# Layer 1's queries: one transposed operand with the high part above the low, and a second one copied from it by DMA

## The chip, the cores and the metric

The kernel runs on one core of one Trainium2 chip. The metric is the device time of one execution in microseconds (us). The engines are TensorE (PE, with its weight loads PEld apart), VectorE (DVE), ScalarE (ACT), GpSimd (POOL) and SyncE (SP), which issues the DMA transfers.

## The reference

A block of two layers works on 512 latent tokens and 256 context tokens of width 1024. Layer 0 is a windowed and a dense grouped-query attention side by side, layer 1 a differential attention; each is followed by a SwiGLU network. The part in question is layer 1's attention, with 8 heads of two halves (`a` = 0, 1) of 64 dimensions:

```python
def heads(p, use_rope):
    q, k, v = jnp.split(p, [qs, 2 * qs], axis=-1)
    q = _rms(q.reshape(b, n, HEADS_C, 2, d), qn)
    k = _rms(k.reshape(b, n, HEADS_C, 2, d), kn)
    if use_rope:
        q, k = _rope(q, cos, sin), _rope(k, cos, sin)
    return q, k, v.reshape(b, n, HEADS_C, 2 * d)
...
s = jnp.einsum('bqhad,bkhad->bhaqk', qb, k).astype(jnp.float32) * scale
p = jax.nn.softmax(s, axis=-1)
a = (p[:, :, 0] - lam * p[:, :, 1]).astype(v.dtype)
return jnp.einsum('bhqk,bkhe->bqhe', a, v)
```

Queries come from the 512 latent tokens, keys and values from all 768.

## The kernel before, in words

All numbers are float32. Where a product must be exact enough, an operand is split into a high part of the faster type `F32R`, which ACT's copy makes, and a low part, the difference; the product is then taken in several terms.

Layer 1's attention works in tiles of 128 tokens (4 latent query tiles, 6 key tiles) and in heads. A head is projected (`Proj1.sums`, with the products at L465) in two half-sums per tile, with weights of 4 units of 256 rows each. `weight1` loads a unit by three transfers (L365, `wir`) into one of two buffers with the tag `raw`, ACT casts its high part (L370, `wih`) and POOL makes its low part (L371, `wil`); five units have room at a time, so a unit's cast waits until PE has used an older one, and a load waits until POOL has finished the unit before the last. All `wir` loads go through SP's queue, which issues in order.

`Proj1.finish` copies a tile's projection out of its accumulator (ACT, L677), normalizes and rotates it, and splits queries (`qd`, L685 on ACT and L686 on DVE) and keys (`kd`, L688 on ACT and L689 on POOL). It returns `transposes`, which is called some steps later: PE turns the queries (L696) and the keys (L702), and ACT copies them out of PSUM (L698, L703). The split key operand `kT` holds the high part in partitions 0 to 63 and the low part in 64 to 127. The query operand `qt` exists twice: once with the high part in both halves of the partitions, once with the low part in both. So the two products L715 and L716 of `attend1` give high x high + high x low and low x high + low x low: all four terms. For this `qd` holds each part twice, and four transposes are made per tile.

`attend1` is a generator with three parts: the scores with the row maximum (L718, `mx`), the exponential (L720, `e`) and the combination of both halves (L727); the transposes of the weights (L734, `ppt`) with copies (L737, L739, `PT`); and the products with the values (L744, `av`) with the normalized output (L746 to L751).

The loop at L1673 goes through 32 pairs of head and query tile. In each pass come the scores of pair i, a half-sum of a later head, the transposes of pair i - 1, another half-sum, the values of pair i - 1, and, as they come due, the transposes of projected tiles (`turned`; a tile comes due five half-sums after its projection, so the queries of a head are turned two to four passes before their use). A tile `qt` has one of five buffers. PE keeps the order in which this is written (`manual_schedule` for PE alone); the instructions of the other engines and of SP's queue are ordered by the framework's planner, from its own estimates.

Of the kernel before, what the change touches and what calls it, by code (L numbers as in the profile page):

```python
# [12 lines left out]
F32R = mybir.dt.float32r  # L13
# [6 lines left out]
P = 128  # L20
# [7 lines left out]
HD = 64  # L28
# [23 lines left out]
def bc(ap, pos, n):  # L52

    dims = [list(d) for d in ap.ap]
    return AP(ap.tensor, ap.offset, dims[:pos] + [[0, n]] + dims[pos:])
# [8 lines left out]
def backbone(es: ExitStack, tc: tile.TileContext, x, c, ctx, c_ctx, mod_w, mod_b, norm_mix_w, norm_ffn_w,  # L64
# [3 lines left out]
    nc = tc.nc  # L68
# [24 lines left out]
    def acc_tile(name, n=512, one=None):  # L93

        if one is None:
            one = turn["acc"] = 1 - turn["acc"]
        return p_1.tile([P, 512], F32, name=name, tag=f"acc{one}")[:, :n]
# [4 lines left out]
    def tr_tile(name, shape, dt=F32, one=None):  # L102
        if one is None:
            one = turn["tr"] = 1 - turn["tr"]
        return p_1.tile(shape, dt, name=name, tag=f"tr{one}")
# [10 lines left out]
    def f32(ap):  # L116
        return ap.bitcast(F32)
# [13 lines left out]
    identr = cp.tile([P, P], F32R, name="identr")  # L131
# [24 lines left out]
    def rsqrt(ss, n, inv, tag):  # L156

        r = small.tile([P, n], F32, name="rs_" + tag, tag="rs_" + tag)
        nc.gpsimd.tensor_scalar(r, ss, inv, EPS, ALU.mult, ALU.add)
        nc.gpsimd.tensor_tensor(r, r, neghalf[:, :n], ALU.pow)  # L160
        return r
# [319 lines left out]
    def weights0(b, wp, subs, new_tile=raw_tile, loads=((0, 1), (), (2,), (3,))):  # L481
# [3 lines left out]
        for u in range(4):  # L485
# [13 lines left out]
            subs[u % len(subs)].tensor_sub(lo, raw, f32(hi))  # L499
            yield hi, lo  # L500

    def tables0(j, tabs, wp):
        tabs[j] = rope_tables(wp, *((ev_qn_a[0], ev_kn_a[0]) if j == 0 else (ev_qn_b[0], ev_kn_b[0])))

# [152 lines left out]
    class Proj1:  # L657
# [14 lines left out]
        def finish(self, t, ps):  # L672

            n, wp, kT, qs = self.width(t), self.wp.pool, self.kT, self.qs
            m, h0 = (n - P) // HD, 0 if t < NTX else 2
            raw = wp.tile([P, 384], F32, name="qkv", tag="qkv", bufs=4)
            nc.scalar.copy(raw[:, :n], ps[:, :n])  # L677
            nc.gpsimd.tensor_copy(self.vv[:, t, :], raw[:, n - P:n])
            y, r = rotate_all(raw[:, :n - P], h0, m, t, self.wc, self.tb, wp)
            nc.gpsimd.tensor_tensor(y, y, bc(r, 2, HD), ALU.mult)  # L680
            nq = m - 2
            if nq:
                qd = wp.tile([P, 2, 2, 2, HD], F32R, name="qd", tag="qd", bufs=3)
                yb = bc(y[:, 0:2], 2, 2)
                nc.scalar.copy(qd[:, 0], yb)  # L685
                nc.vector.tensor_sub(qd[:, 1], yb, f32(qd[:, 0]))  # L686
            kd = wp.tile([P, 2, 2, HD], F32R, name="kd", tag="kd", bufs=3)
            nc.scalar.copy(kd[:, :, 0, :], y[:, nq:nq + 2])  # L688
            nc.gpsimd.tensor_sub(kd[:, :, 1, :], y[:, nq:nq + 2], f32(kd[:, :, 0, :]))  # L689

            def transposes():
                if nq:
                    pt = tr_tile("qpt", [P, 2, 2, P], F32R)
                    for j in range(2):
                        for a in range(2):
                            nc.tensor.transpose(pt[:, j, a, :], qd[:, j, a].rearrange("p a d -> p (a d)"), identr)  # L696
                    qt = self.qp.tile([P, 2, 2, P], F32R, name="qt", tag="qt", bufs=5)
                    nc.scalar.copy(qt, f32(pt))  # L698
                    qs[t] = qt
                pk = tr_tile("kpt", [P, 2, P], F32R)  # L700
                for a in range(2):
                    nc.tensor.transpose(pk[:, a, :], kd[:, a].rearrange("p a d -> p (a d)"), identr)  # L702
                nc.scalar.copy(kT[:, :, t * P:(t + 1) * P], f32(pk))  # L703
            return transposes

    def attend1(h, t, state, o_t, nlam, subln, mp):
        qs, kT, vv = state.qs, state.kT, state.vv
        mx = small.tile([P, 2], F32, name="mx", tag="mx")
        sm = small.tile([P, 2], F32, name="sm", tag="sm")
        E = []  # L710
        for a in range(2):
            sc = p_sc.pool.tile([P, 1024], F32, name="sc", tag="sc", bufs=2)
            for s0, k0, k1 in ((256, SEQ, TOK), (512, 0, SEQ)):
                so = sc[:, s0:s0 + k1 - k0]
                nc.tensor.matmul(so, qs[t][:, 0, a, :], kT[:, a, k0:k1], start=True, stop=False)  # L715
                nc.tensor.matmul(so, qs[t][:, 1, a, :], kT[:, a, k0:k1], start=False, stop=True)  # L716
            s = sc[:, 256:256 + TOK]
            nc.vector.tensor_reduce(mx[:, a:a + 1], s, AX.X, ALU.max, negate=True)  # L718
            e = mp.tile([P, TOK], F32, name="e", tag="e", bufs=PBUF)
            turn["exp"] = nc.scalar.activation(e, s, AF.Exp, bias=mx[:, a:a + 1], accum_out=sm[:, a:a + 1])  # L720
            E.append(e)
        rc = small.tile([P, 2], F32, name="rc", tag="rc")
        nc.vector.reciprocal(rc, sm)

        rt = small.tile([P, 1], F32, name="rt", tag="rt")
        nc.vector.scalar_tensor_tensor(rt, sm[:, 0:1], nlam, rc[:, 1:2], ALU.mult, ALU.mult)
        nc.vector.scalar_tensor_tensor(E[0], E[1], rt, E[0], ALU.mult, ALU.add)  # L727
        yield
        vt = [4, 5, 0, 1, 2, 3]
        pts = []  # L730
        for g0, m in ((0, 4), (4, 2)):
            pt = tr_tile("ppt", [P, 4, P])
            for a in range(m):
                nc.tensor.transpose(pt[:, a, :], E[0][:, (g0 + a) * P:(g0 + a + 1) * P], ident)  # L734
            PT = mp.tile([P, 4, P], F32, name="PT", tag="PT", bufs=3)
            if g0:
                nc.vector.tensor_copy(PT[:, :m], pt[:, :m])  # L737
            else:
                nc.scalar.copy(PT, pt)  # L739
            pts += [PT[:, a, :] for a in range(m)]  # L740
        yield
        av = acc_tile("av", P, one=1)
        for kc, PT in enumerate(pts):
            nc.tensor.matmul(av, PT, vv[:, vt[kc], :], start=kc == 0, stop=kc == NT - 1)  # L744
        oc = o_t[t][:, h * P:(h + 1) * P]
        nc.scalar.activation(oc, av, AF.Copy, scale=rc[:, 0:1])  # L746
        ss = small.tile([P, 1], F32, name="oss", tag="oss")
        o1 = mp.tile([P, P], F32, name="o1", tag="o1", bufs=2)
        nc.scalar.activation(o1, oc, AF.Square, accum_out=ss)
        r = rsqrt(ss, 1, 1.0 / P, "o")  # L750
        nc.vector.scalar_tensor_tensor(oc, oc, r, subln, ALU.mult, ALU.mult)  # L751
# [405 lines left out]
    wp = Pool("mw0", "right")  # L1157
# [5 lines left out]
    for t in CTX_FIRST:  # L1163
# [4 lines left out]
        for g in range(2):  # L1168
            pt = tr_tile("npt", [P, 4, P])
# [120 lines left out]
    if True:  # L1290
        for i, (b, t) in enumerate(steps):
            j = i % NT
# [37 lines left out]
            if t == 0:  # L1330
# [13 lines left out]
                wp = Pool("w0", "right")  # L1344
# [219 lines left out]
    wp = Pool("mw1", "right")  # L1564
# [44 lines left out]
    if True:  # L1609
# [117 lines left out]
        wp = Pool("w1", "right")  # L1727
# [203 lines left out]
```

## Time and profile before

| | before |
|---|---|
| median of 3 runs (lowest to highest) | 1695.23 us (1695.23 to 1698.65) |
| the profiled execution: its span (no other time of it is given) | 1695.6 us |
| mean granted clock of TensorE | 0.992 |
| TensorE busy | 1631.5 us, 96% |
| layer 1's attention, from its first scores to the last | 1002.2 to 1293.5 us |
| SP's loads inside 1010 to 1250 us | 63 of 128 KB |

Busy time of the engines is the time in which they execute; matmuls overlap one another, so the distance of their starts, not the length of one, says what one costs. In a group's row stand its line, engine, operation, output and inputs, the shape, the count, the busy time, the mean length in ns, and the idle time before it with what ended it. In a row of the timeline stand the start, the length, the engine and the line; "x4" merges four neighbours, and brackets hold idle time before it. A row of the waits gives total, number and longest.

### The profile page before, as it was taken

The page shows a single profiled execution, that of the slowest core. Times are in us where ns is not written, and L with a number is a line of the kernel's source. Part 1 is how long each engine was busy: PE and PEld are TensorE (multiplying, and loading weights), DVE is VectorE, ACT ScalarE, POOL GpSimd, SP SyncE. Part 2 cuts the span into 40 slices and gives each one's busy share as a digit, 9 for nine tenths or more (in the row PEclk, how much of TensorE's full clock was granted, in tenths as well). Part 3 has the DMA queues.
Part 4 walks back from the last instruction along what each step waited for, and adds up shares of the span by engine and source line. Part 5 has one row for each costly group of instructions (what it writes and reads, how often), then busy time and mean ns, then how long its engine had stood idle before and what let it go on. Part 6 is the DMA issues. An engine that isn't in the chain of part 4 may idle for free. (4 is left out here: it accounts for less than half of the span.)

```text
span 1695.6 us, 28585 instructions
## 1 busy us (share of the span) xinstructions
PE 1631.5 (96%) x10390; PEld 1468.6 (87%) x10390; DVE 1146.7 (68%) x2014; ACT 937.0 (55%) x2011; POOL 696.4 (41%) x867
## 2 busy tenths in 40 slices
PE   6999999899999999999999989999999999999998
PEld 3977787677999999998777889999988899999887
DVE  3765656754799887767767656666666598887434
ACT  5565555745456665545554456666666555555320
POOL 2665554321346554412413366666664242221000
PEclk8999999999999999999999999999999999999999
DMA  9222221411455555439966311111112433331431
GB/s 319 69 71 74 70 70 50 164 60 38 129 167 172 164 159 162 134 108 347 296 184 189 99 43 38 48 42 44 50 45 97 125 93 102 111 101 57 137 99 62
DMA packets 218108, 194.64 MB, mean 115 GB/s; under 512 B 20016, under 2 KB 202864, under 8 KB 217968
## 3 DMA queue, kind: packets, MB, share of 16 engines
q1 hardware_dynamic: 217616, 192.62, 36.8%
q8 instruction: 81, 1.33, 0.3%
q14 instruction: 59, 0.48, 0.1%
q10 hardware_dynamic: 352, 0.21, 0.0%
HBM read 179.92 MB, written 12.87 MB: 114 GB/s over the span
## 5 line engine op out<-in xcount | busy, mean ns | idle before, releaser
L901 ACT CAST wbh<-wr 128x512 fp32r<-128x512 f32 x170 | 104.9, 621 | 130.2 <-PE p L933 73.4
L933 PE MATMUL p<-hT,wbh 128*128 128x256 f32 (+1 forms) x752 | 154.5, 299 | 0.0
L465 PE MATMUL inps<-wih,hT 128*128 128x384 f32 x512 | 144.2, 344 | 7.3 <-ACT qkv L677 7.3
L911 POOL TENSOR_TENSOR wbl<-wr,wbh 128x512 fp32r<-128x512 f32 x43 | 60.0, 1396 | 173.6 <-ACT wbh L901 173.6
L933 PEld LDWEIGHTS p<-hT,wbh 128*128 128x128 f32 x752 | 121.9, 191 | 0.2
L911 DVE TENSOR_TENSOR wbl<-wr,wbh 128x512 fp32r<-128x512 f32 x127 | 107.7, 858 | 21.0 <-ACT wbh L901 16.8
L933 PE MATMUL p<-hT,wbl 128*128 128x256 f32 (+1 forms) x376 | 111.9, 298 | 0.0
L933 PE MATMUL p<-t,wbh 128*128 128x384 f32 (+1 forms) x480 | 111.3, 318 | 0.0
L604 POOL TENSOR_SCALAR Pt<-Pt,rc 128x256 f32<-128x256 f32 (+3 forms) x96 | 74.6, 788 | 89.3 <-DVE rc L601 83.1
L231 POOL TENSOR_TENSOR modp<-modp 128x512 f32<-128x512 f32 x40 | 57.4, 1436 | 114.3 <-ACT modp L230 114.3
L465 PEld LDWEIGHTS inps<-wih,hT 128*128 128x128 f32 x512 | 93.3, 188 | 10.6 <-ACT qkv L677 9.7
L933 PE MATMUL p<-hTt,wbh 128*128 128x256 f32 (+1 forms) x480 | 101.0, 302 | 0.0
L887 POOL TENSOR_TENSOR wr<-wr 128x512 f32<-128x512 f32 x40 | 61.6, 1540 | 89.8 <-DVE ws L892 85.8
L933 PE MATMUL p<-b,wbh 128*128 128x384 f32 x368 | 93.8, 336 | 0.2 <-DVE c L961 0.2
L901 ACT CAST wbh<-ws 128x512 fp32r<-128x512 f32 x120 | 69.4, 579 | 43.1 <-PE p L933 29.0
L224 DVE SCALAR_TENSOR_TENSOR ma<-modw,cols,ma 128x256 f32<-128x256 f32 x140 | 89.2, 637 | 2.3
L592 ACT ACTIVATE Pt<-sc,nm 128x256 f32<-128x256 f32 (+3 forms) x96 | 67.6, 707 | 35.3 <-DVE nm L588 16.9
L465 PE MATMUL inps<-wil,hT 128*128 128x384 f32 x256 | 86.0, 336 | 0.0
L933 PEld LDWEIGHTS p<-t,wbh 128*128 128x128 f32 x480 | 82.9, 189 | 0.0
L911 DVE TENSOR_TENSOR wbl<-ws,wbh 128x512 fp32r<-128x512 f32 x120 | 81.7, 681 | 1.7 <-ACT wbh L901 1.6
L933 PEld LDWEIGHTS p<-hTt,wbh 128*128 128x128 f32 x480 | 78.3, 191 | 3.1 <-ACT modp L230 1.6
L230 ACT ACTIVATE modp<-modw,cols 128x256 f32<-128x256 f32 x160 | 68.4, 500 | 18.0 <-POOL ma L236 10.1
(355 smaller groups left out, 5217.9 us busy)
## 6 DMA issues: line engine op xcount, KB each, us to landing
modw<-in_mod_w_dram SPq DMA_DIRECT2D x96, 512.0 KB, 5.2
wr<-in_ffn_w_in_dram SPq DMA_DIRECT2D x176, 256.0 KB, 2.9
wdr<-in_ffn_w_out_dram SPq DMA_DIRECT2D x66, 512.0 KB, 3.7
wir<-in_od_w_in_dram SPq DMA_DIRECT2D x96, 128.0 KB, 2.3
hidm<-hid SPq DMA_DIRECT2D x44, 192.0 KB, 1.9
hr<-hidm SPq DMA_DIRECT2D x22, 192.0 KB, 3.5
x<-in_x_dram SPq DMA_DIRECT2D x8, 512.0 KB, 3.5
wir<-in_ev_w_in_dram SPq DMA_DIRECT2D x16, 256.0 KB, 3.5
```

The costliest lines, as they stand in the source:

```text
L224: nc.vector.scalar_tensor_tensor(acc, w[:, k], scale[k], acc, ALU.mult, ALU.add)
L230: nc.scalar.activation(pr[:, k], w[:, k], AF.Copy, scale=scale[k])
L231: nc.gpsimd.tensor_add(pr[:, 0:2], pr[:, 0:2], pr[:, 2:4])
L465: nc.tensor.matmul(ps, hs[j][:, k, :], ws[k // 2][z][:, k % 2, c0:c1], start=(k, j, z) == (0, 0, 0), stop=(k, j, z) == (KT - 1, 1, 0))
L592: turn["exp"] = nc.scalar.activation(p[:, :n], s, AF.Exp, bias=nm[:, c1], accum_out=sm[:, c1])
L604: nc.gpsimd.tensor_scalar(p[:, :n], p[:, :n], rc[:, hh:hh + 1], 1.0, ALU.mult, ALU.mult)
L887: nc.gpsimd.tensor_sub(w, raw[f, "G1"], w)
L901: nc.scalar.copy(hi, w)
L911: (nc.gpsimd if name == "G2" else nc.vector).tensor_sub(lo, raw[need[n]], f32(hi))
L933: nc.tensor.matmul(ps, w[:, k, :], H[b][h][:, k, :], start=first and k == 0 and q == 0, stop=final and k == 3 and q == 2, skip_group_check ...
```

## The change

`qd` now holds each query once, its high part in the first 64 and its low part in the last 64 columns, as `kd` always did. Two transposes per tile, one for each half-head, give the first operand, `qt[:, 0]`, with high above low. The second operand, `qt[:, 1]`, has low above high; two DMA transfers on SP's queue copy it from the first inside SBUF, each moving 64 partitions of 1 KB (64 KB). The products stay the same two: high x high + low x low, and low x high + high x low.

A swap isn't issued where the tile is turned but one tile later: `halves_swapped` keeps the newest one back, and `swapped()` at the start of each pair's scores issues what is left.

```diff
+    swaps = []
+
+    def swapped(left=0):
+        while len(swaps) > left:
+            to, src = swaps.pop(0)
+            for j in range(2):
+                nc.sync.dma_start(f32(to[HD * (1 - j):HD * (2 - j)]), f32(src[HD * j:HD * (j + 1)]))
+
+    def halves_swapped(to, src):
+        swaps.append((to, src))
+        swapped(1)
...
-                qd = wp.tile([P, 2, 2, 2, HD], F32R, name="qd", tag="qd", bufs=3)
-                yb = bc(y[:, 0:2], 2, 2)
-                nc.scalar.copy(qd[:, 0], yb)
-                nc.vector.tensor_sub(qd[:, 1], yb, f32(qd[:, 0]))
+                qd = wp.tile([P, 2, 2, HD], F32R, name="qd", tag="qd", bufs=3)
+                nc.scalar.copy(qd[:, :, 0, :], y[:, 0:2])
+                nc.vector.tensor_sub(qd[:, :, 1, :], y[:, 0:2], f32(qd[:, :, 0, :]))
...
-                    pt = tr_tile("qpt", [P, 2, 2, P], F32R)
-                    for j in range(2):
-                        for a in range(2):
-                            nc.tensor.transpose(pt[:, j, a, :], qd[:, j, a].rearrange("p a d -> p (a d)"), identr)
+                    pt = tr_tile("qpt", [P, 2, P], F32R)
+                    for a in range(2):
+                        nc.tensor.transpose(pt[:, a, :], qd[:, a].rearrange("p a d -> p (a d)"), identr)
                     qt = self.qp.tile([P, 2, 2, P], F32R, name="qt", tag="qt", bufs=5)
-                    nc.scalar.copy(qt, f32(pt))
+                    nc.scalar.copy(qt[:, 0], f32(pt))
+                    halves_swapped(qt[:, 1], qt[:, 0])
                     qs[t] = qt
...
         E = []
+        swapped()
         for a in range(2):
```

On PE nothing moves: two query transposes stand wherever four stood. The planner orders the other engines anew. On SP's queue, in the passes of the middle heads, the loads of the weight units stood in a row before (the number behind `wir` is one unit's buffer: 12389 is unit 3 of one head, 12921 to 12945 are units 0 to 3 of the next):

```order
L365 DMA wir_12381<-in_od_w_in_dram 128x2x128 x3
L365 DMA wir_12389<-in_od_w_in_dram 128x2x128 x3
L365 DMA wir_12921<-in_od_w_in_dram 128x2x128 x3
L365 DMA wir_12929<-in_od_w_in_dram 128x2x128 x3
L365 DMA wir_12937<-in_od_w_in_dram 128x2x128 x3
```

Now the swaps of the query tiles (L508, a pair for each tile) stand between them:

```order
L365 DMA wir_12381<-in_od_w_in_dram 128x2x128 x3
L508 DMA qt_12029<-qt_12029 64x256 x2
L365 DMA wir_12389<-in_od_w_in_dram 128x2x128
L508 DMA qt_12289<-qt_12289 64x256 x2
L365 DMA wir_12389<-in_od_w_in_dram 128x2x128 x2
L508 DMA qt_12332<-qt_12332 64x256 x2
L365 DMA wir_12921<-in_od_w_in_dram 128x2x128 x3
L365 DMA wir_12929<-in_od_w_in_dram 128x2x128 x3
L508 DMA qt_12470<-qt_12470 64x256 x2
L365 DMA wir_12937<-in_od_w_in_dram 128x2x128 x3
L508 DMA qt_12585<-qt_12585 64x256 x2
```

Unit 3's load is split by the swap of the next head's query tile 0, and unit 0 follows behind that of tile 1. On ACT, at the same place of a middle head, stood before (the first `wih` here is unit 3's cast, the second that of unit 0 of the head after):

```order
L420 ACTIVATE sq<-qkv 128x256
L370 CAST wih<-wir 128x768
L720 ACTIVATE e,sm<-sc,mx 128x768
L685 CAST qd<-qy 128x256
L688 CAST kd<-qy 128x2x64
L370 CAST wih<-wir 128x768
L739 COPY PT<-ppt 128x512
L720 ACTIVATE e,sm<-sc,mx 128x768
L677 COPY qkv<-inps 128x256
```

and now stands, with the lines of the changed file (11 to 12 higher):

```order
L420 ACTIVATE sq<-qkv 128x256
L370 CAST wih<-wir 128x768
L732 ACTIVATE e,sm<-sc,mx 128x768
L696 CAST qd<-qy 128x2x64
L699 CAST kd<-qy 128x2x64
L751 COPY PT<-ppt 128x512
L732 ACTIVATE e,sm<-sc,mx 128x768
L370 CAST wih<-wir 128x768
L689 COPY qkv<-inps 128x256
```

The copy of PT and the second exponential moved ahead of the second cast.

## The prediction

> **What bounds the kernel now.** I read the page's first block first, then the busy time by stretch around the changed place.
>
> ```profile
> span 1695.6 us, 28585 instructions
> PE 1631.5 (96%) x10390; PEld 1468.6 (87%) x10390; DVE 1146.7 (68%) x2014; ACT 937.0 (55%) x2011; POOL 696.4 (41%) x867
> ```
>
> TensorE (PE) is busy in 96% of the span. The change touches only layer 1's attention; its three stretches (start, six even heads, end) are, with the columns PE, PEld, DVE, ACT and POOL busy, granted clock, DMA share and GB/s:
>
> ```profile
> 975.00:1010.00 35.00, 29.80 (x194) 27.91 (x193) 17.85 (x35) 19.19 (x48) 24.66 (x39) 1.00 0.19 52
> 1010.00:1250.00 240.00, 234.42 (x1657) 225.68 (x1656) 151.80 (x312) 157.47 (x409) 159.79 (x254) 1.00 0.15 42
> 1250.00:1300.00 50.00, 44.50 (x286) 39.13 (x285) 37.81 (x68) 35.43 (x82) 30.48 (x48) 0.97 0.31 95
> ```
>
> In the middle 240 us PE idles only 5.6 us, at full clock; every other engine is at two thirds, and the DMA engines at 15%. So time goes where PE instructions go, except where PE already waits. The waits of that middle stretch (total, times, longest):
>
> ```profile
> PEld inps L465 <- ACT qkv L677: 4.8, 6, 0.9
> PE inps L465 <- ACT qkv L677: 3.4, 6, 0.6
> PEld inps L465 <- POOL wil L371: 2.6, 6, 1.2
> ACT wih L370 <- PE inps L465: 4.8, 12, 0.6
> ACT wih L370 <- DMA wir<-in_od_w_in_dram: 2.6, 2, 1.4
> PE av L744 <- ACT PT L739: 0.7, 2, 0.6
> ```
>
> Both of PE's recurring waits come six times, once per head: one for the copy of the projection out of its accumulator, one for the low part of a weight unit. The second decides what a saved PE instruction is worth.
>
> **The PE term.** The timeline of PE in one head:
>
> ```profile
> 1098.51 0.54 PE L696 MATMUL qpt<-identr,qd 128*128 128x128 f32 x4
> 1098.88 0.33 PE L702 MATMUL kpt<-identr,kd 128*128 128x128 f32 x2
> 1099.05 0.41 PE L465 MATMUL inps<-wih,hT 128*128 128x384 f32 x1
> ...
> 1101.20 0.47 PE L696 MATMUL qpt<-identr,qd 128*128 128x128 f32 x4
> 1101.50 0.34 PE L702 MATMUL kpt<-identr,kd 128*128 128x128 f32 x2
> 1101.67 0.35 PE L715 MATMUL sc<-kT,qt 128*128 128x256 f32 x1
> ```
>
> Matmuls overlap, so the cost is start to start: four query transposes take 0.37 and 0.30 us, two key transposes behind them 0.17. Dropping two of four saves 0.15 (half of 0.30) to 0.185 (half of 0.37); I take 0.165. With 8 heads of 4 query tiles that is 32 x 0.165 = 5.3 us (4.8 to 5.9) if every group lay on the path. The Trainium skill ("TensorE: Matmul & The Clock Gate", section "Wait — 56ns, not 53.3ns?") has back-to-back matmuls of 128 columns 56 ns apart at full clock; by it, an estimate, the 64 would be 3.6 us. The trace does not agree here: 0.17 for two is 85 ns each, and the row decides.
>
> **Half of it is already owed to a wait.** Each head's four groups come at about 1098.5, 1101.2, 1109.1 and 1118. Behind the first two, PE meets this:
>
> ```profile
> 1105.45 0.40 PE L465 MATMUL inps<-wih,hTc 128*128 128x256 f32 x2
> 1105.69 0.28 PE L465 MATMUL inps<-wil,hTc 128*128 128x256 f32 x1
> 1105.81 0.39 PE L465 MATMUL inps<-wih,hTc 128*128 128x256 f32 x2
> 1106.29 0.39 PE L465 MATMUL inps<-wil,hTc 128*128 128x256 f32 x1
> ...
> 1107.73 1.60 PE L744 MATMUL av<-vv,PT 128*128 128x128 f32 x12 [0.58 <-ACT PT L739]
> ```
>
> Two products take 0.24 us (1105.45 to 1105.69); the next two take 0.48, so 0.24 is idle, since the low part of weight unit 3 ends at 1104.39 + 1.85 = 1106.24. POOL, busy with six short operations and unit 2 between them, runs without a pause from unit 1 to unit 3:
>
> ```profile
> 1097.32 1.98 POOL L371 TENSOR_TENSOR wil<-wir,wih 128x768 fp32r<-128x768 f32 x1 [1.92 <-ACT wih L370]
> ...
> 1104.39 1.85 POOL L371 TENSOR_TENSOR wil<-wir,wih 128x768 fp32r<-128x768 f32 x1
> ```
>
> Its start waits for ACT's cast, and that cast for PE to give back a weight buffer (the 12 waits in the list above), before the two groups; the order of POOL between these two rows is unchanged. So 2 x 0.165 saved in front of that wait only lengthens it. What counts is the other two groups: 6 heads x 0.33 = **2.0 us**.
>
> **What ACT and DVE give.** Groups of the attention stretch (busy, mean ns):
>
> ```profile
> L698 ACT CAST qt<-qpt 128x512 fp32r<-128x512 f32 x32 | 18.7, 586 | 2.7 <-PE qpt L696 2.6
> L703 ACT CAST kT<-kpt 128x256 fp32r<-128x256 f32 x48 | 18.2, 378 | 1.2 <-PE kpt L702 1.2
> L685 ACT CAST qd<-qy 128x256 fp32r<-128x256 f32 x32 | 13.0, 406 | 23.4 <-POOL qy L680 23.4
> L688 ACT CAST kd<-qy 128x128 fp32r<-128x128 f32 x46 | 13.7, 298 | 14.4 <-POOL qy L680 14.2
> L427 DVE TENSOR_TENSOR qy<-qkv,rc 128x128 f32<-128x128 f32 x14 | 4.7, 339 | 3.0 <-POOL kd L689 1.5 <-issue 0.6 <-POOL vv L678 0.5
> ```
>
> The copy of qt goes from 586 to 378 ns, the cast of qd from 406 to 298: 0.316 x 32 = 10 us of ACT, nearly all in idle time. On a path to PE lies the DVE subtraction between a tile's two row maxima, which sets the second exponential and then the accumulator copy that PE awaits:
>
> ```profile
> 1092.34 0.41 DVE L686 TENSOR_TENSOR qd<-qy,qd 128x256 fp32r<-128x256 f32 x1
> ```
>
> At half the elements it is like the 339 ns row or a little under: 0.1 less, once per head, 6 x 0.1 = **0.6 us**. The new order also puts ACT's copy of PT ahead of the cast of the next head's first unit, which waits for its DMA; that was the 0.58 us in the row at 1107.73 and the whole entry of 0.7: **0.7 us**.
>
> **The two ends.** Three waits there:
>
> ```profile
> 992.39 0.37 PE L702 MATMUL kpt<-identr,kd 128*128 128x128 f32 x2 [0.86 <-POOL kd L689]
> 1002.13 0.28 PE L288 MATMUL gps<-cst,modc 128*8 128x128 f32 x1 [0.41 <-ACT kT L703]
> 1269.79 0.75 PE L696 MATMUL qpt<-identr,qd 128*128 128x128 f32 x4 [0.76 <-ACT qt L698]
> ```
>
> Head 0's groups mostly precede waits on POOL (0.86), and their saving is lost as above; ACT's shorter copy in front of the wait at 1002.13 (0.21) and its group (0.17) count, with the shorter cast of qd (0.11) twice: 0.6. Head 7's four groups give 0.66, and 0.21 at 1269.79, where PE waits for the copy of qt itself; some goes into the latencies of the last tiles: 0.7. Together **1.3 us**. Gains: 2.0 + 0.6 + 0.7 + 1.3 = 4.6.
>
> **What is added.** Each tile issues two transfers of 64 KB on SP's queue: 64 in all. Latency first:
>
> ```profile
> L715 PE MATMUL sc<-kT,qt x128: 274/378/400, 1002.2 to 1293.5; 128*128 128x256 f32 x64, 128*128 128x512 f32 x64
> L698 ACT CAST qt<-qpt x32: 573/587/594, 989.4 to 1270.6; 128x512 fp32r<-128x512 f32 x32
> L365 SPq DMA_DIRECT2D wir<-in_od_w_in_dram x63: 367/469/1345, 1020.0 to 1220.9; - x63
> DMA to landing us min/median/max: 2.1/2.3/4.0
> ```
>
> The first copy ends near 990 and its scores begin at 1002.2; score steps are (1293.5 - 1002.2) / 31 = 9.4 us apart, and in the even heads a tile is turned two to three steps ahead of its use, over 20 us. Against that stand two issues (0.94) and 2.3, at worst 4.0, us to landing. The latency is hidden, with 7 us left at the tightest place; without that cover it would be about 3 us x 32. The Trainium skill ("DMA: Bandwidth & Descriptors", section "Anatomy of one DMA — SWDGE (gpsimd) path") speaks against many small transfers: about 2 us fixed for each (fitted there on GpSimd's queue), an estimate of 2.15 us for 64 KB. The 2.3 us of the 128 KB loads agrees; exposed, it would be 32 x 2.15 = 69 us.
>
> What stands behind these issues in SP's queue are the weight loads, and the new order splits unit 3: one load, the two swap issues of query tile 0, the other two loads.
>
> ```profile
> 1099.33 1.40 SPq L365 DMA_DIRECT2D wir<-in_od_w_in_dram  x3
> ...
> 1099.09 0.59 ACT L698 CAST qt<-qpt 128x512 fp32r<-128x512 f32 x1
> ...
> 1102.84 0.85 ACT L370 CAST wih<-wir 128x768 fp32r<-128x768 f32 x1
> ```
>
> The first load is out at 1099.7; the copy of qt, now 0.38, ends at 1099.47, so SP waits for nothing, and the two others move back by two issues, 0.85 us (0.37 and 0.47). The third was issued at 1099.33 + 1.40 - 0.47 = 1100.26 and by 2.3 landed at 1102.55, before its cast; now 1103.4. The cast then ends at 1104.25, and POOL is free for its subtraction at 1104.39: the slack in the landing is 1.0 us, and 0.85 of it is used. No cost at the median, and up to 0.85 a head when the landing is late, as the ACT row of the waits (2 times, up to 1.4) shows it can be. Bounds: 0 and 6 x 0.85 = 5.1; I take **0.5 us**, near the low end, since only two casts in that stretch waited for a load at all. Unit 0 of the next head also moves behind tile 1's swap, but its cast now stands two ACT instructions later. The two added waits of one score product per tile have no row; between 0 and 32 x 0.03 (the length of a semaphore instruction, seen at 0.02 to 0.03 on the queues, an estimate), I take 0.
>
> **Sum.** 4.6 - 0.5 = 4.1 us. The profiled span of 1695.6 becomes 1691.5; the median, 0.4 below the span, goes from 1695.23 to **1691.1**. A change of 0.2% (3.4 us) is about what a measurement can tell; the three runs before are two equal and one 3.4 above.
>
> **Rivals.**
> - *All 32 groups count.* If POOL's chain moves forward with PE, nothing is owed to the wait: 5.3 + 0.6 + 0.7 + 0.6 (ACT at the ends) - 0.2 = 7.0, 1688.2 us. For it: PE at 98%. Against: the 0.24 us, six times.
> - *Eaten.* The swaps' data and issues take unit 3's slack: 0.5 a head, 6 x 0.5 = 3.0 and 4.6 - 3.0 = 1.6 gained, 1693.6 us. For it: only 0.15 us of slack is left, and the late landings.
> - *Slower: SP's queue as the bound.* If an issue inside SBUF costs what the slowest load's did (1.345 us), the pair takes 2.7; less 1.0 of slack, PE waits 1.7 more per head, 6 x 1.7 = 10.2, net 5.6 lost, 1700.8 us. It outweighs the gain from a delay of 1.0 + 4.6 / 6 = 1.8 us on. For it: SP issues in order, and its wait for a copy holds all that follows. Against: a median of 0.47. The Trainium skill, the page and section just named, says that semaphore waits happen on the issuing sequencer; that is this mechanism, and SP's in-order rows agree.
> - That the change does not do what it says can be ruled out: PE's new order has two query transposes wherever four stood, and is otherwise the same.
>
> **Chances.** Forecast 0.45, all count 0.16, eaten 0.27, slower 0.12. The forecast lies just past the 0.2% bound; four fifths of it I count as faster: 0.36 + 0.16 = 0.52. Same: 0.09 + 0.27 = 0.36. Slower 0.12. The range runs from 1687.5 (all count, with 5.9 for the groups) to 1696.5 (eaten, with the full 0.85 a head: 0.5 lost, and rounding up); it leaves out the slower rival and little else. The forecast's own range is 1690 to 1692.5.
>
> **What would show it.** Right: 64 query transposes instead of 128, PE's wait on unit 3's low part longer by about 0.3 us per head, the wait on PT gone, no score product waiting for a transfer, unit 3's cast at most 0.6 us later. Wrong: score products with idle time ended by a DMA; swap issues of over 0.8 us; the wait on unit 3 longer by over 0.8 (eaten or slower), or not longer at all (all count).

## The result, and the profile after

The changed kernel takes 1699.93 us (median of 9 runs, 1698.12 to 1703.45), the kernel before, measured beside it, 1695.23 us (9 runs, 1692.44 to 1698.65): ratio 1.003, 95% interval 1.0019 to 1.0041. It is slower by some 5 us where 4 us less were forecast, and lies outside the range given. The profiled execution was the slowest of the nine (1703.45 us).

The page's first block, as shown of before:

```profile
span 1701.7 us, 28605 instructions
PE 1629.8 (96%) x10326; PEld 1467.0 (86%) x10326; DVE 1153.3 (68%) x2014; ACT 925.9 (54%) x2011; POOL 695.9 (41%) x867
```

The 64 transposes are gone (10390 to 10326), and PE's busy time fell by 1.7 us while the span grew by 6.1. Not all of that growth is the change's: layer 1's scores begin at 1004.0 us instead of 1002.2, and layer 0 is untouched. The three stretches of layer 1's attention:

```profile
975.00:1010.00 35.00, 29.39 (x189) 27.68 (x188) 16.79 (x35) 17.68 (x46) 24.75 (x39) 1.00 0.29 81
1010.00:1250.00 240.00, 228.97 (x1579) 219.83 (x1580) 155.75 (x308) 144.80 (x400) 155.62 (x251) 0.99 0.20 55
1250.00:1300.00 50.00, 44.65 (x285) 40.15 (x283) 35.74 (x66) 34.20 (x84) 31.89 (x50) 0.93 0.31 96
```

In the middle 240 us PE now idles 11.0 us; it was 5.6. The waits of that stretch say on what:

```profile
PEld inps L465 <- POOL wil L371: 9.0, 6, 1.7
PE inps L465 <- POOL wil L371: 7.8, 6, 1.5
PEld inps L465 <- ACT qkv L689: 5.7, 12, 0.7
ACT wih L370 <- issue: 5.7, 3, 2.1
ACT wih L370 <- DMA wir<-in_od_w_in_dram: 5.6, 3, 2.5
PE inps L465 <- ACT qkv L689: 3.0, 8, 0.5
```

The wait of the weight loads on unit 3's low part was 2.6 us, six times; it is 9.0, again six times. No score product waits for a transfer, and the wait on PT (0.7) is gone. The timeline of the same head as before shows where the 6.4 us arise (SP, ACT, POOL and PE). Unit 1's cast is the anchor; in the trace of before it is this one:

```profile
1096.41 0.83 ACT L370 CAST wih<-wir 128x768 fp32r<-128x768 f32 x1 [0.59 <-PE inps L465]
```

And in the changed kernel:

```profile
1098.66 0.84 ACT L370 CAST wih<-wir 128x768 fp32r<-128x768 f32 x1 [0.59 <-PE inps L465]
...
1101.65 0.37 SPq L365 DMA_DIRECT2D wir<-in_od_w_in_dram  x1
...
1102.12 1.10 SPq L508 DMA_DIRECT2D qt<-qt  x2
...
1103.28 1.12 SPq L365 DMA_DIRECT2D wir<-in_od_w_in_dram  x2
...
1106.42 0.83 ACT L370 CAST wih<-wir 128x768 fp32r<-128x768 f32 x1 [1.60 <-DMA wir<-in_od_w_in_dram]
...
1107.34 1.82 POOL L371 TENSOR_TENSOR wil<-wir,wih 128x768 fp32r<-128x768 f32 x1 [0.64 <-PE ppt L746]
...
1107.72 0.39 PE L465 MATMUL inps<-wih,hTc 128*128 128x256 f32 x2
1109.21 0.38 PE L465 MATMUL inps<-wil,hTc 128*128 128x256 f32 x1 [1.09 <-POOL wil L371]
```

Count from unit 1's cast. Unit 3's third load goes out 5.24 us after it (in the trace of before 3.85), its cast starts after 7.76 (before 6.43) and now waits for the load, POOL's subtraction starts after 8.68 (before 7.98), and PE waits longer: two products that otherwise take 0.24 us from start to start took 0.48 before and take 1.49 now (1107.72 to 1109.21), so the wait grew from 0.24 to 1.25 us. POOL stood idle in front of this subtraction; the row puts that down to PE, but ACT's cast ended last, at 1107.25. In all six heads of this stretch ACT stands idle in front of unit 3's cast, for 1.5 to 2.5 us, until 2.4 to 3.0 us after the issue of the third load; the list above puts three of these waits down to the load and leaves three open ("issue").

For the comparison of all kernels below I take the first score product of each of the 32 steps from the timeline, and compare the distances of these steps with those of before. So layer 0's scatter (the scores begin between 997 and 1004 us, in kernels that don't differ there) drops out. Summed over the heads, by the place in the head (query tile 0 to 1, 1 to 2, 2 to 3, 3 to the next head's 0), in us against before:

| | 0-1 | 1-2 | 2-3 | 3-0 | sum | median us (runs), before beside it | ratio, 95% interval |
|---|---|---|---|---|---|---|---|
| changed | -0.1 | -3.9 | +7.4 | +0.9 | +4.3 | 1699.93 (9), 1695.23 | 1.0030, 1.0019 to 1.0041 |
| no_swaps | 0.0 | -3.8 | +1.3 | +2.5 | +0.1 | 1696.18 (12), 1694.45 | 1.0005, 0.9993 to 1.0016 |
| late_swaps | 0.0 | -3.8 | +1.1 | -1.0 | -3.7 | 1692.82 (12), 1694.45 | 0.9986, 0.9975 to 0.9996 |
| extra_swaps | 0.0 | -0.2 | +1.7 | +4.0 | +5.5 | 1700.52 (9), 1694.45 | 1.0035, 1.0023 to 1.0047 |
| act_queue | +0.2 | -1.5 | +20.4 | +5.8 | +24.9 | 1722.22 (4), 1694.45 | 1.0156, 1.0142 to 1.0170 |
| thin_swaps | 0.0 | -3.9 | +9.3 | +1.4 | +6.8 | 1699.34 (12), 1695.11 | 1.0020, 1.0010 to 1.0031 |
| own_before | 0.0 | -0.2 | +0.8 | +0.9 | +1.5 | 1697.73 (11), 1695.11 | 1.0008, 0.9999 to 1.0017 |
| own_after | +0.7 | -3.6 | +4.8 | +2.5 | +4.4 | 1700.04 (12), 1695.11 | 1.0025, 1.0014 to 1.0035 |
| own_no_swaps | +0.7 | -3.7 | +2.4 | +4.1 | +3.5 | 1697.94 (11), 1695.11 | 1.0014, 1.0001 to 1.0026 |
| no_swaps_ordered | 0.0 | -3.9 | +1.4 | +0.4 | -2.1 | 1692.98 (11), 1694.61 | 0.9987, 0.9977 to 0.9998 |
| before_with_t0 | 0.0 | +0.3 | +2.8 | +2.7 | +5.8 | 1702.02 (6), 1694.61 | 1.0037, 1.0024 to 1.0050 |
| before_late_64 | 0.0 | -0.2 | -0.5 | +2.2 | +1.5 | 1695.91 (12), 1694.61 | 1.0000, 0.9989 to 1.0012 |
| late_dve | 0.0 | -3.9 | +1.3 | +7.2 | +4.7 | 1698.60 (11), 1694.61 | 1.0016, 1.0007 to 1.0026 |

The ratios are not simply quotients of the two medians. The medians of thin_swaps and of the runs beside the second round (1695.11) each take in one run that was far slower than all the others (4057.57 and 2651.05 us), which the ratios leave out.

The sums hold a scatter of about 1 us that has nothing to do with the edits. In the last two heads the granted clock falls in before as well, and how long it stays low differs between the profiles: from 1262 to 1284 us its mean is 0.92 in before and in late_swaps, 0.84 in no_swaps_ordered and in before_late_64. For the six even heads alone the sums are +3.3 for the changed kernel, -4.0 for late_swaps, -3.9 for no_swaps_ordered and +0.4 for before_late_64.

The wait on unit 3 lies in 2-3. The changed kernel gains 3.9 us in 1-2, where two of a head's four groups of transposes stand and where PE's wait on the copy of a projection became shorter, here in the head shown, before and in the changed kernel:

```profile
1095.07 0.44 PE L465 MATMUL inps<-wih,hT 128*128 128x384 f32 x1 [0.61 <-ACT qkv L677]
```

```profile
1097.31 0.44 PE L465 MATMUL inps<-wih,hT 128*128 128x384 f32 x1 [0.34 <-ACT qkv L689]
```

It loses 7.4 in 2-3. The heads don't lose alike there. The head shown loses only 0.03, mainly since its wait of 0.58 on PT is gone; another loses 0.4, since one of its loads had been late in the trace of before too; four lose 0.6 to 1.1 each, and one alone 3.3. In that one the two loads behind the swap took 2.11 us to issue, 1 us more than in the head shown, and PE waited accordingly:

```profile
1183.78 2.11 SPq L365 DMA_DIRECT2D wir<-in_od_w_in_dram  x2
...
1190.61 0.39 PE L465 MATMUL inps<-wil,hTc 128*128 128x256 f32 x1 [1.51 <-POOL wil L371]
```

The trace of before has slow issues as well (up to 1.345 us). Behind this wait the granted clock fell (the column behind POOL's):

```profile
1188.00:1190.00 2.00, 0.88 (x6) 0.48 (x4) 0.79 (x3) 2.00 (x6) 1.25 (x1) 1.00 0.66 190
1190.00:1192.00 2.00, 1.39 (x11) 1.39 (x12) 1.28 (x4) 2.00 (x5) 1.83 (x4) 0.95 0.17 50
1192.00:1194.00 2.00, 2.00 (x13) 2.00 (x13) 2.00 (x2) 1.00 (x5) 2.00 (x2) 0.50 0.57 166
1194.00:1196.00 2.00, 2.00 (x14) 2.00 (x14) 1.15 (x3) 1.33 (x6) 1.75 (x6) 0.70 0.14 33
```

From 1188 to 1192 PE was busy for 2.27 of 4 us, and in the next 4 us it had 0.50 and 0.70 of its clock: another 1.6 us, an estimate (2 x 0.50 + 2 x 0.30). The profile is that of the slowest run, but thin_swaps, profiled near its median, has such a head too; how often it happens isn't known. The Trainium skill ("TensorE: Matmul & The Clock Gate", section "Part 1: The HAM clock gate") has the clock at one half after an idle window of about 3.4 us; the 0.50 agrees, but here PE was not idle for a whole window.

### The profile page after: what moved, and what is told of

Read it like the earlier page. It is cut to its first block, busy times and chain, and to the rows that moved or that the text cites. A ratio compares the mean times of both kernels' runs of the same rounds, so it can differ in the third digit from the quotient of the medians.

```text
span 1701.7 us, 28605 instructions
## 1 busy us (share of the span) xinstructions
PE 1629.8 (96%) x10326; PEld 1467.0 (86%) x10326; DVE 1153.3 (68%) x2014; ACT 925.9 (54%) x2011; POOL 695.9 (41%) x867
## 5 line engine op out<-in xcount | busy, mean ns | idle before, releaser
L465 PE MATMUL inps<-wihi,hT 128*128 128x384 f32 x256 | 76.4, 356 | 1.7 <-DVE modc L276 1.5
```

The lines of the kernel that those rows point to most:

```text
L465: nc.tensor.matmul(ps, hs[j][:, k, :], ws[k // 2][z][:, k % 2, c0:c1], start=(k, j, z) == (0, 0, 0), stop=(k, j, z) == (KT - 1, 1, 0))
```

## The experiments

Theory A: the issues of the transfers, ahead of unit 3's loads in SP's queue, make unit 3 late. Theory B: the bytes moved inside SBUF beside the loads cost, wherever they are issued. Theory C: the shorter transposes are worth nothing, or the new order of the planner costs.

**First round: take the transfers away, delay them, add them alone, move them.** Without transfers:

```diff
-                    halves_swapped(qt[:, 1], qt[:, 0])
...
-                nc.tensor.matmul(so, qs[t][:, 1, a, :], kT[:, a, k0:k1], start=False, stop=True)
+                nc.tensor.matmul(so, qs[t][:, 0, a, :], kT[:, a, k0:k1], start=False, stop=True)
```

> The changed kernel without its 64 transfers; the second score product uses the first operand again, so the high x low terms are left out and the high x high ones counted twice. Theory A (the swaps stand ahead of two of unit 3's three loads in SP's queue, POOL's low part of unit 3 ends later and PE waits for it): 4 to 5 us below the kernel before, PE's wait on unit 3's low part back to about 0.3 to 0.6 us a head (0.24 before, plus the saved transposes). Theory B (the transfers cost through their own traffic on the DMA engines, wherever they are issued): the same here. Theory C (the shorter transposes and the planner's new order of ACT, DVE and POOL bring the loss): 3 us or more above the kernel before, with the waits of the changed kernel.

Measured: 1696.18 us, no difference from before that the interval shows. The loss in 2-3 fell from 7.4 to 1.3 and PE's wait on unit 3 from 7.8 to 3.2 us, as A and B say, but 3-0 rose to +2.5, and the 4 us of gain that both expected did not come. C was alive.

The same transfers, issued one pass later:

```diff
     def halves_swapped(to, src):
-        swaps.append((to, src))
-        swapped(1)
+        kept.append((to, src))
+
+    def pass_begins(first):
+        if not first:
+            swapped()
+        swaps.extend(kept)
+        kept.clear()
+        if first:
+            swapped()
...
-        swapped()
+        pass_begins(h == 0 and t == 0)
```

> The swaps are issued one pass of scores later; in SP's queue unit 3's three loads then stand together ahead of the swaps of query tiles 0 and 1, with as many transfers as in the changed kernel. Theory A: 2 to 4.5 us below the kernel before, unit 3's cast again about 6.4 us after unit 1's, PE's wait for its low part 0.3 to 0.7 us a head. Theory B: as slow as the changed kernel, 3 us or more above the kernel before. Theory C: as slow as the changed kernel.

Measured: 1692.82 us, ratio 0.9986 (0.9975 to 0.9996): faster than both kernels, by a little, and at the low end of what A expected. Its timeline in the same head (unit 1's cast at 1095.14) shows unit 3's three loads together, the transfers of two tiles behind them:

```profile
1098.14 1.40 SPq L365 DMA_DIRECT2D wir<-in_od_w_in_dram  x3
...
1099.64 2.38 SPq L508 DMA_DIRECT2D qt<-qt  x4
...
1101.45 0.83 ACT L370 CAST wih<-wir 128x768 fp32r<-128x768 f32 x1
...
1103.17 1.83 POOL L371 TENSOR_TENSOR wil<-wir,wih 128x768 fp32r<-128x768 f32 x1
...
1105.05 0.39 PE L465 MATMUL inps<-wil,hTc 128*128 128x256 f32 x1 [0.45 <-POOL wil L371]
```

The cast starts 6.31 us after unit 1's and hardly waits for its load (0.14 us), the subtraction after 8.03, and PE's wait is 0.45. All 64 transfers are still there, so B falls, and so does C in its plain form: shorter transposes and transfers together gain 3.7 us of attention here. The planner ordered ACT, DVE and POOL anew in this kernel, too, so the place of the transfers isn't the only difference from the changed one.

The kernel before, with the transfers added into a tile that nothing reads:

```diff
                     nc.scalar.copy(qt, f32(pt))
+                    spare = self.qp.tile([P, 2, P], F32R, name="spare", tag="spare", bufs=2)
+                    halves_swapped(spare, qt[:, 0])
```

> The kernel before with its four transposes and its whole copy, and in addition the 64 transfers, into a spare tile that nobody reads: the added cost alone. Theory A: the loss without the gain, 6 x (1.0 to 1.4) us, 6 to 8 us above the kernel before, if the planner splits unit 3's loads in the same way. Theory B: 6 to 8 us above as well. Theory C: within 2 us of the kernel before.

Measured: 1700.52 us, 6.1 above the kernel before, with 5.5 lost in the attention, as A and B expected. PE's wait on unit 3 rose from 1.0 to 4.2 us, but only 1.7 of the loss stands in 2-3 and 4.0 in 3-0, where the planner had also changed the order of ACT. This run alone did not prove A.

The transfers issued from ACT's queue:

```diff
-                nc.sync.dma_start(f32(to[HD * (1 - j):HD * (2 - j)]), f32(src[HD * j:HD * (j + 1)]))
+                nc.scalar.dma_start(f32(to[HD * (1 - j):HD * (2 - j)]), f32(src[HD * j:HD * (j + 1)]))
```

> The changed kernel with the 64 transfers issued from ACT's queue instead of SP's; ACT then spends the issue time (about 0.5 us each) and the planner orders it around that. Theory A: SP's loads of unit 3 go out together again, but its cast stands behind the issues on ACT: between 3 us below and 2 us above the kernel before, and PE's wait for unit 3 follows ACT's cast. Theory B: 3 us or more above. Theory C: 3 us or more above.

Measured: 1722.22 us, far above what A had expected (between 3 us below and 2 us above the kernel before). Unit 3's loads are as early as ever (the third 3.93 us after unit 1's cast), but its cast comes 8.69 after it. The tile's row and the wait of the middle stretch:

```profile
L508 ACTq DMA_DIRECT2D qt<-qt x64: 468/488/941, 987.4 to 1295.7; - x64
```

```profile
PE inps L465 <- POOL wil L371: 16.2, 6, 2.7
```

Each issue holds ACT for 0.49 us, and ACT's casts and exponentials stand behind it. In four heads the granted clock fell as well (a mean of 0.72 over 6 us each). The cost lies with the engine that issues. The Trainium skill ("DMA: Bandwidth & Descriptors", section "Issuing engines are not separate DMA queues") says that the time a sequencer takes to initiate a transfer is usually small relative to the transfer. Here it is 0.59 us on SP against 2.0 us to landing, and this small part sets the time, since the rest is hidden.

**Second round: bytes or issues, and a buffer to free the loads.** The change with thin transfers, every instruction in the same order on each engine:

```diff
-                nc.sync.dma_start(f32(to[HD * (1 - j):HD * (2 - j)]), f32(src[HD * j:HD * (j + 1)]))
+                nc.sync.dma_start(f32(to[HD * (1 - j):HD * (2 - j), :, 0:8]), f32(src[HD * j:HD * (j + 1), :, 0:8]))
...
-                nc.tensor.matmul(so, qs[t][:, 1, a, :], kT[:, a, k0:k1], start=False, stop=True)
+                nc.tensor.matmul(so, bc(qs[t][:, 1, a, 0], 1, P), kT[:, a, k0:k1], start=False, stop=True)
```

> The changed kernel with the same 64 transfers in the same order on every engine, each cut to 8 of 128 columns (4 KB instead of 64 KB; the second product uses one swapped column for all 128). Theory A (what costs is the place of the issues in SP's queue, ahead of unit 3's loads): the issues stay, so the time stays within 1.5 us of the changed kernel's 1699.9, the last load of unit 3 still goes out 5.2 us after unit 1's cast and PE waits some 7 to 8 us on unit 3's low part. Theory B (the bytes moved beside the loads cost): the 4 to 5 us go, 1695 to 1696, with unit 3's loads out sooner or landing sooner.

Measured: 1699.34 us; the wait on unit 3 stays (7.5 us). The issues of the changed kernel, 64 KB each:

```profile
L508 SPq DMA_DIRECT2D qt<-qt x64: 461/587/1672, 991.8 to 1278.2; - x64
```

and those of the thin ones, 4 KB each:

```profile
L508 SPq DMA_DIRECT2D qt<-qt x64: 590/597/1237, 985.4 to 1274.3; - x64
```

With a sixteenth of the bytes an issue takes as long, and so does the kernel. B is out. (In this profile, too, one head had the clock at 0.50, and 4.5 us of its 9.3.)

Then a buffer of its own for unit 3's load, so that it need not wait for unit 1's subtraction, in the changed kernel, its twin without transfers, and the kernel before:

```diff
+    def own_raw(shape, name):
+        return at.pool.tile(shape, F32, name=name, tag="raw3", bufs=1)
+
...
-            new_head([weight1(h, u, wh, nc.gpsimd) for u in range(4)])
+            new_head([weight1(h, u, wh, nc.gpsimd, own_raw if u == 3 else raw_tile) for u in range(4)])
```

> The changed kernel, and unit 3 of each head loads into a buffer of its own, so its loads no longer wait for unit 1's subtraction and no longer queue behind a swap issue that is as late as they are. The order of ACT, PE and POOL is the same as in the twin without transfers. Theory A: PE's wait on unit 3's low part falls from 7.8 us to below 2, and the transfers then cost under 1 us against the twin without them; 4 to 6 us below the twin of the kernel before, about 1689 to 1691. Theory B: 4 to 5 us above the twin without transfers.

> The twin of the former without the transfers (the second product reuses the first operand, so the products of high and low parts are left out). Theory A: within 1 us of the one with transfers. Theory B: 4 to 5 us below it. Theory C (the shorter transposes are worth nothing here): both as long as the twin of the kernel before.

> The kernel before, with four transposes a tile, and a buffer of its own for unit 3. The wait on unit 3's low part was 1.0 us in the trace of PE by itself (0.24 a head with the pipelined ones), so 1 to 3 us below the kernel before: 1691.5 to 1693.5. Theory A expects the changed twins 4 to 6 us below this one, since now all 32 groups of transposes count (32 x 0.165 = 5.3); theory C none of it.

Measured: 1700.04, 1697.94 and 1697.73 us. None is faster than before, and the expectation of 4 to 6 us between the twins fell. PE's wait on unit 3 is gone in all three, but another has come. In the changed twin:

```profile
PE qpt L706 <- DVE qd L697: 3.7, 3, 1.3
PE av L756 <- ACT PT L751: 3.2, 3, 1.9
```

and in the twin of before:

```profile
PE qpt L696 <- DVE qd L686: 4.8, 5, 1.0
```

POOL's timeline in the latter, with unit 1's cast at 1054.32, has unit 3's subtraction ahead of the scaling of a tile's queries (L680), which came first in the kernel before:

```profile
1060.81 1.85 POOL L371 TENSOR_TENSOR wil<-wir,wih 128x768 fp32r<-128x768 f32 x1
...
1063.06 0.61 POOL L680 TENSOR_TENSOR qy<-qy,rs_q 128x256 f32<-128x256 f32 x1
```

With the load early, the planner lets POOL subtract 6.5 us after unit 1's cast instead of 8.0, the queries are scaled later, and their transposes wait. The load was not the only thing in front of PE there: POOL's 1.85 us has to go somewhere.

The two changed twins, with the same order on ACT, PE and POOL, lie 2.1 us apart by their medians, where A expected less than 1; their intervals overlap. What the transfers still delay in own_after is the load of the next head's unit 0, for which ACT's cast now waits in five heads:

```profile
ACT wih L370 <- DMA wir<-in_od_w_in_dram: 10.6, 5, 3.5
```

and in own_no_swaps:

```profile
ACT wih L370 <- DMA wir<-in_od_w_in_dram: 0.4, 2, 0.2
```

**Third round: the order of ACT, and sixteen transfers alone.** In the traces of the first round one thing differed where no_swaps lost its 2.5 us in 3-0: in one pass of four ACT ran both exponentials before the copy of a projection. In no_swaps:

```profile
1070.14 0.90 ACT L731 ACTIVATE e<-sc,mx 128x768 f32<-128x768 f32 x1
...
1071.03 0.90 ACT L731 ACTIVATE e<-sc,mx 128x768 f32<-128x768 f32 x1
...
1071.91 0.37 ACT L689 COPY qkv<-inps 128x256 f32<-128x256 f32 x1
...
1072.33 0.45 PE L465 MATMUL inps<-wih,hT 128*128 128x384 f32 x1 [0.46 <-ACT qkv L689]
```

In late_swaps and before, and in five of the six even heads of the changed kernel, the copy stands between the two. Theory D: that order ate the gain. The run without transfers again, with the second exponential of that pass held behind the copy (`turn["qkv"]` is the last such copy):

```diff
+        def apart(i):
+            return i % 4 == 3 and i < last - 1
...
+            if a and apart:
+                yield
...
-            turn["exp"] = nc.scalar.activation(e, s, AF.Exp, bias=mx[:, a:a + 1], accum_out=sm[:, a:a + 1])
+            with behind(*(("qkv",) if a and apart else ())):
+                turn["exp"] = nc.scalar.activation(e, s, AF.Exp, bias=mx[:, a:a + 1], accum_out=sm[:, a:a + 1])
...
             step()
+            if apart(i):
+                next(attend[i])
```

> The changed kernel without transfers once more (products of high and low parts left out), with one thing put in order by hand: in one pass of four the second exponential is issued behind ACT's copy of the projection, as in the kernels before, changed and with late transfers; in the run without transfers the planner had put it ahead. Theory D (that order ate the shorter transposes' gain there: 0.65 us a head between the fourth and fifth score step, five or six heads): 3 to 4 us less than without the order, about 1692.5 to 1693.5, like the kernel with late transfers. Theory C (the shorter transposes are worth nothing): still 1695 to 1696.

Measured: 1692.98 us, ratio 0.9987 (0.9977 to 0.9998). The same place:

```profile
1070.14 0.90 ACT L737 ACTIVATE e<-sc,mx 128x768 f32<-128x768 f32 x1
...
1071.26 0.37 ACT L689 COPY qkv<-inps 128x256 f32<-128x256 f32 x1
...
1071.52 0.91 ACT L737 ACTIVATE e<-sc,mx 128x768 f32<-128x768 f32 x1
...
1071.68 0.45 PE L465 MATMUL inps<-wih,hT 128*128 128x384 f32 x1
```

PE goes on 0.65 us earlier, and 3-0 falls from +2.5 to +0.4. D holds. Without transfers and with this order the kernel is as fast as with late transfers (1692.98 and 1692.82): transfers behind the loads cost nothing that shows.

The kernel before with only query tile 0's pair of each head, 16 transfers, the order of ACT held the same way, so that in the even heads it is that of before:

```diff
+                    if t == 0:
+                        spare = self.qp.tile([P, 2, P], F32R, name="spare", tag="spare", bufs=2)
+                        halves_swapped(spare, qt[:, 0])
```

> The kernel before, four transposes a tile, with only query tile 0's two transfers of each head (16 of 64) going into a spare tile, behind the first load of unit 3 and ahead of its other two; ACT's order held as in the kernel before. Theory A: these 16 alone carry the cost, 0.4 to 0.9 us a head: 2 to 5 us above the kernel before, 1697.5 to 1700, with PE's wait on unit 3's low part up from 1.0 to 3 or more. Theory B (every transfer costs alike): a quarter of the 5.5 us that 64 cost in the other run, 1.4.

Measured: 1702.02 us, ratio 1.0037 (1.0024 to 1.0050), above the range that A gave. Sixteen transfers cost as much as all 64 (5.8 and 5.5 us of attention). Its timeline, with unit 1's cast at 1098.38:

```profile
1101.16 0.37 SPq L365 DMA_DIRECT2D wir<-in_od_w_in_dram  x1
...
1101.66 1.11 SPq L508 DMA_DIRECT2D spare<-qt  x2
...
1105.88 0.83 ACT L370 CAST wih<-wir 128x768 fp32r<-128x768 f32 x1 [0.95 <-DMA wir<-in_od_w_in_dram]
...
1106.79 1.84 POOL L371 TENSOR_TENSOR wil<-wir,wih 128x768 fp32r<-128x768 f32 x1 [0.40 <-ACT wih L370]
```

The cast is at 7.50 instead of 6.43 and waits for its load in every head; PE's wait on unit 3 rose from 1.0 to 4.1 us. Half of the loss stands in 2-3, the other half in 3-0, where PE's waits on the copy of the projection rose from 3.4 to 5.3 us. The planner also changed the order of DVE, and moved POOL's subtraction of the next head's unit 0 behind one more operation in this kernel, so how much of that second half is the late load itself and how much the order it led to stays open.

And all 64 transfers in the kernel before, issued one pass later as in late_swaps, with the order held:

```diff
+    def halves_swapped(to, src):
+        kept.append((to, src))
...
+                    spare = self.qp.tile([P, 2, P], F32R, name="spare", tag="spare", bufs=2)
+                    halves_swapped(spare, qt[:, 0])
...
+        pass_begins(h == 0 and t == 0)
```

> The kernel before with all 64 transfers into a spare tile, issued one pass later, so behind unit 3's loads; the second exponential held behind the copy of the projection as in the kernel before. Theory A: unit 3's cast as early as before and no cost from the transfers: 1694 to 1695.5. Theory B: 4 to 5 us above the kernel before, as with the transfers ahead of the loads (1700.5).

Measured: 1695.91 us, ratio 1.0000 (0.9989 to 1.0012). Unit 3's loads go out first, and its cast, with unit 1's at 1094.33, is at 6.43 as before:

```profile
1097.11 1.40 SPq L365 DMA_DIRECT2D wir<-in_od_w_in_dram  x3
...
1098.61 1.11 SPq L508 DMA_DIRECT2D spare<-qt  x2
...
1100.76 0.84 ACT L370 CAST wih<-wir 128x768 fp32r<-128x768 f32 x1
```

So the same 64 transfers show no cost behind the loads (the interval leaves room for 2 us either way), and with 16 of them ahead of two loads the kernel is 6 us slower. The planner's order of ACT, DVE and POOL differs between these two kernels as well, so not all of the 6 us is shown to be the place's. What is shown, in the changed kernel and in this one, is the chain from the late load over the cast and the subtraction to PE, in each of the six heads. A stands, B does not.

Last, an attempt to go further: late_swaps with unit 3's low part made on DVE.

```diff
-            new_head([weight1(h, u, wh, nc.gpsimd) for u in range(4)])
+            new_head([weight1(h, u, wh, nc.vector if u == 3 else nc.gpsimd) for u in range(4)])
```

> The kernel with late transfers, with unit 3's low part made on DVE instead of POOL. If POOL's queue in front of that subtraction is what PE still waits for there (3.2 us, six times), the wait goes and with it 1 to 3 us: 1690 to 1692. Rival: on DVE it stands in front of a row maximum or a rotation, and the wait moves to the copy of the projection or to the transposes: 1693 to 1695.

Measured: 1698.60 us. The rival had the mechanism, though not the time, which is above its range: the wait on the low part fell to 1.8 us, and the one on the copy of the projection rose from 2.3 us in late_swaps to 9.2:

```profile
PE inps L465 <- ACT qkv L698: 9.2, 13, 1.6
```

## Why the prediction was wrong, point by point

- *Two transposes less save 0.165 us a group*: right. From the first query transpose to the key transposes behind it, the groups went from 0.30 and 0.38 to 0.13 and 0.21 us.
- *Half of it is owed to the wait on unit 3*: right. In late_swaps the two groups in front of that wait bring PE 0.28 us closer to it in the head shown, and the wait grows by 0.36 (0.24 to 0.60, from start to start); over the six heads the wait of the weight loads on unit 3 went from 2.6 to 4.4 us.
- *What ACT and DVE give*: PT's wait went, as said. The path over the second exponential is there too, but it was sized at 0.1 us a head, and PE's wait on the copy fell by 0.27 in the head shown. The subtraction itself fell from 0.41 to 0.28 us there; where the other half comes from stays open. Without the cost of the transfers 3.3 us were forecast for the six even heads; late_swaps gains 4.0.
- *The two ends*: the 1.3 us forecast there did not show. From head 6 on late_swaps takes 0.3 us longer than before, and ahead of the first scores layer 0's scatter hides what there may be.
- *Latency of the transfers hidden, the added waits nothing*: right. No score product waits for a transfer, and late_swaps and before_late_64 show no cost for 64 of them.
- *The step that failed* is the one on SP's queue: "the two others move back by two issues, 0.85 us", with a landing slack of 1.0, and a cost of 0.5 us in all. The place was right, the size was not. An issue inside SBUF took 0.59 us at the median, not 0.37 and 0.47: the pair moved what followed by 1.16 us (1102.12 to 1103.28), the loads beside it went out slower too, and the third load was late by 1.39. It landed 2.5 us after its issue, not 2.3. Both together are 1.6 us, against the slack of 1.0 read from the trace of before: POOL started 0.70 us late, and PE, which came 0.28 earlier by what it had saved, waited 1.0 longer. The cast was late in each of the six heads, not only in those with a late landing. The cost put at 0.5 us came to some 7 over these heads (+3.3 here against -4.0 in late_swaps, whose planned order differs as well).
- *The bounds of that cost*, 0 and 6 x 0.85, left out what follows a longer wait: in one head, where an issue was slow besides, the clock fell, and that head alone lost 3.3 of the 7.4 us, about half of it (the 1.6) by the clock. The upper bound of the range, 1696.5, also stands 0.8 above its own sum (1695.23 + 0.5), and the result lies beyond it all the same.
- *The slower rival* was the right mechanism with a wrong price. It asked for a pair of 2.7 us and put the turning point at a delay of 1.8 us; it happened with 1.4, or 1.6 with the later landing. I took an issue of a load from DRAM as the nearest row to one inside SBUF, and took the slack as if nothing else moved. A kernel with 0.15 us of slack left by its own sum should have had more than 0.12 for this side.
- *What would show it*: the criterion for "eaten or slower", a wait on unit 3 longer by over 0.8 us, was met in the head shown (1.0), and over six heads it is 6.4 / 6 = 1.07.
- *Not foreseen at all*: that the order which the planner gives ACT is worth nearly as much as the change. The copy of a projection before or behind one exponential is 0.65 us a head; it hid the gain in no_swaps. In extra_swaps it stands where most of the loss is, but before_with_t0 loses there too with the good order, so that share stays open. In the changed kernel itself the order was the good one in all but one head.

## What to carry to other kernels

When a transfer is added to an in-order queue, count what stands behind it, by the issue time of its own kind, and hold the sum against the landing slack of the next load that a busy engine needs; the bytes may cost nothing that shows while the issue does. Issue such transfers behind the loads that are due, as late as their reader allows: with the same 64 transfers the changed kernel was 5 us slower or 2 us faster than before, by their place and by the order that the planner made around it. And where a planner orders the other engines, compare twins in the same order before crediting a difference to the edit, and look for the new wait when one is taken away.

## What was not expected of the hardware

- An issue on SP's queue inside SBUF takes 0.59 us at the median with 64 KB and 0.60 us with 4 KB; in the kernels with the transfers behind the loads it is 0.57 (late_swaps) and 0.51 (before_late_64). The loads from DRAM have a median of 0.47. From ACT's queue it takes 0.49 us.
- Pauses of PE of 1.7 us in all within 4 us were followed by a granted clock of 0.50, then 0.70, in the next 4 us.
